# Attention's transposes taken two blocks of keys at a time: runs of eight, and one split of 1024 columns for two of 512

## The chip, the cores and the metric

The kernel runs on one core of one Trainium2 chip. The metric is the device time of one execution in microseconds (us), taken several times; the median counts.

## What is computed

A model of three stages: an attention block with its feed-forward network, a long-convolution block with its own, and a second block of a state-space branch and a pooling branch. Everything is float32. The change touches the attention alone, with 16 heads, 512 query rows and 768 keys (256 of a context, 512 of the sequence):

```python
def one_block(qblk):
    s = jnp.einsum('bqhd,bkhd->bhqk', qblk, k).astype(F32) * scale
    p = jax.nn.softmax(s, axis=-1).astype(v.dtype)
    return jnp.einsum('bhqk,bkhd->bqhd', p, v)
```

The queries and keys have 96 numbers per head, the values 64. The output of the heads is multiplied by `mla_w_o` and added to `x`; the kernel's later stages are the same before and after the change.

## The kernel before

Engines: PE is TensorE (matmuls and transposes), ACT is ScalarE, DVE is VectorE, and SP's queue issues the loads. A float32 operand of a matmul is split into a high part (ACT copies it to `fp32r`) and a low part (DVE subtracts the high part); the helper is `split`, and its two instructions carry the lines 262 (ACT) and 263 (DVE). A product takes three matmuls (lines 266 to 268) or, with packed values, two.

Per head `h` the attention does this:

- `proj_q`, `proj_k`, `proj_v` make the operands of later heads, in the PSUM tile `pj_pj` (one buffer, tag `pj`).
- `score(h, i)` makes the scores of 128 queries against 768 keys in `pss` (tag `sc`, two buffers of 1024 columns), takes the row maximum on DVE (line 890), the exponential on ACT (892), the reciprocal on DVE (893) and scales on ACT (897). The result is `p`, with queries on the partitions.
- `trans(h, j)` turns the block `j` of 128 keys, for the four blocks of queries: four PE transposes into the tile `pst` of 512 columns (tag `tr`, two buffers), and then `split` into `pth` and `ptl` (three buffers each). There are six blocks of keys per head.
- `pv_(h, j)` multiplies the packed values `v` with `pth` (line 914) and with `ptl` (915) into `pso` (tag `pso`), and after the last block adds the halves (919 on ACT, 920 on DVE).

The word list `STEPS` sets the order in which a head's calls are made: `s0` is `score(h+1, 0)`, `q0` the projection of a later head, `t2` is `trans(h, 2)`, `o3` is `pv_(h, 3)`, `M0` one call of `mod_row`. `mod_row` (line 385) belongs to another stage: it loads a row block `mr` of 512 KB, which SP issues, and reduces it on DVE (line 388); 24 such rows are put into the attention. `PPLAN` is the list for the first projections, with a letter for the PSUM tag each one uses.

The calls are traced in that order, and a scheduler then orders each engine's instructions by priority and by a model of when an operand is ready, so a later call's matmuls can stand between those of an earlier one. On the chip each engine works through its row in order and waits at semaphores.

From the last heads on, matmuls of the output projection (`ps_r`, with `h_wo`) stand among those of the attention.

Of the kernel before, what the change touches and what calls it, by code (L numbers as in the profile page):

```python
# [9 lines left out]
F32 = mybir.dt.float32  # L10
F32R = mybir.dt.float32r
# [7 lines left out]
L = 512  # L19
# [165 lines left out]
MR0 = [0] * 4  # L185
MR = [2] * 12 + [0]
XV, XK = 9, 9
PPLAN = "k1o k0t v0p S0 v2s v1s B0 E0 v5p q0s v3o q1t s0 v4p s1 s2 s3"
QPLAN = "a0 a1 k0 g0 r0 g1 y0 e1 e0 e2 l1 R0 g2 l0 Z0 z0 Y0 g3 l2"
STEPS = "s0 q0 t0 k0 t1 s1 o0 t2 o1 t3 o2 t4 M0 s2 o3 v0 t5 k1 v1 s3 M1 v2 x0 o4 o5"  # L190
PLAN = """F I9 F L0 L1 X0 X1 F m1 L2 L3 V F q0 q1 X2 X3 m3 F L4 L5 q2 q3 X4 X5 m5 F L6 L7 q4 q5 X6 X7 m7 F O0 q6 q7 S L8 L9 m9 R c0 F L10 L11 n0 n1 n2 n3
m11 L12 L13 n4 n5 n6 n7 m13 L14 L15 d0 F d1 W0 W1 W2 m15 O1 p0 d2 C0 C1 p1 F c1 C2 C3 d3 p2 K C4 C5 p3 d4 C6 C7 F p4 Q0 Q1 d5 Q2 Q3 p5 d6 Q4 Q5 Q6 Q7 p6 d7 T p7 U
N0 N1 N2 N3 D0 D1 N4 N5 D2 D3 N6 N7 D4 D5 D6 D7 F"""
# [2 lines left out]
def build(nc, tc, A, dbg=None):  # L196
    dbg = dbg or {}
    es = ExitStack()
    pe, act, dve = nc.tensor, nc.scalar, nc.vector
# [11 lines left out]
    ident = const.tile([128, 128], F32, name="ident")  # L211
# [17 lines left out]
    def opool(es_, name, bufs, **kw):  # L229
        kw["reuse_waits"] = "tile"  # L230
        return es_.enter_context(tc.tile_pool(name=name, bufs=bufs, **kw))
# [29 lines left out]
    def split(dsthi, dstlo, src):  # L261
        act.activation(dsthi, src, AF.Copy)  # L262
        dve.tensor_tensor(out=dstlo, in0=src, in1=dsthi.bitcast(F32), op=ALU.subtract)  # L263
# [118 lines left out]
    def gain(dst, sc, g):  # L382
        dve.scalar_tensor_tensor(out=dst, in0=sc, scalar=1.0, in1=g, op0=ALU.add, op1=ALU.mult)

    def mod_row(mpool, cb, n):
        raw = mpool.tile([128, 1024], F32, name="mr", tag="mr", bufs=2)
        nc.sync.dma_start(out=raw, in_=A["modT"][n - 16])
        dve.tensor_tensor_reduce(raw, raw, cb, 1.0, 0.0, ALU.mult, ALU.add, mods[:, n:n + 1])  # L388

# [3 lines left out]
    def load_cb(mpool):  # L393
        cb = mpool.tile([128, 1024], F32, name="cb")
        nc.sync.dma_start(out=cb, in_=A["crow"].broadcast_to([128, 1024]))
        act.activation(cb, cb, AF.Silu)
        return cb
# [11 lines left out]
    x0 = [rp.tile([128, L], F32, name=f"x0_{k}") for k in range(KT)]  # L409
# [8 lines left out]
    pp = opool(es_a, "pp0", 4, space=PSUM)  # L418
# [333 lines left out]
    rowp = opool(es_a, "row0", 1)  # L752
    cb = load_cb(rowp)
    rows = list(range(16, 40))
# [77 lines left out]
    pp = opool(es_ps, "ppa", 1, space=PSUM)  # L832
    ap_ = opool(ph, "ap", 2)
    rowp = opool(es_row, "rowp", 1, side="right")
    cb = load_cb(rowp)
    O = [op_.tile([128, L], F32, name=f"O{k}") for k in range(KT)]
    vt, Qt, Pt, Tt, Ot = {}, {}, {}, {}, {}

    def pjt(tag):
        return pp.tile([128, 1024 if tag == "sc" else L], F32, name="pj_" + tag, tag=tag, bufs=2 if tag in ("sc", "tr") else 1)[:, :L]  # L840

    def proj_v(qr, j, tag="pj"):
        uvh, uvl = wuv.block(qr)
        ps = pjt(tag)
        js = slice(j * 128, (j + 1) * 128)
        for k in range(2):
            w = slice(k * 256, (k + 1) * 256)
            pe.matmul(ps[:, :256], ckh[k][:, js], uvh[:, w], start=(k == 0), stop=False)
            pe.matmul(ps[:, :256], ckl[k][:, js], uvh[:, w], start=False, stop=False)
            pe.matmul(ps[:, :256], ckh[k][:, js], uvl[:, w], start=False, stop=(k == 1))  # L850
        v = ap_.tile([128, 4, 2, 64], F32R, name="v", bufs=12)
        p3 = ps[:, :256].rearrange("p (h d) -> p h d", h=4)
        act.activation(v[:, :, 0, :], p3, AF.Copy)
        dve.tensor_tensor(out=v[:, :, 1, :], in0=p3, in1=v[:, :, 0, :].bitcast(F32), op=ALU.subtract)
        vt[qr, j] = v

    def proj_k(h, part, tag="pj"):
        cs = (slice(0, L), KC)[part]
        w_ = cs.stop - cs.start
        psk = pjt(tag)  # L860
        for k in range(2):
            mm3(psk[:, :w_], wuk.unit(h + k), (ckh[k][:, cs], ckl[k][:, cs]), k == 0, k == 1)
        for e in range(2):
            b = (h + e) % 3
            act.activation(Kh[b][0:64, cs], psk[64 * e:64 * e + 64, :w_], AF.Copy)
            dve.tensor_tensor(out=Kl[b][0:64, cs], in0=psk[64 * e:64 * e + 64, :w_],
                              in1=Kh[b][0:64, cs].bitcast(F32), op=ALU.subtract)

    def proj_q(h, tag="pj"):
        psq = pjt(tag)  # L870
        chunk(psq, wuq, h * 4, cq, FULL)
        Qh = ap_.tile([128, L], F32R, name="Qh")
        Ql = ap_.tile([128, L], F32R, name="Ql")
        qf = ap_.tile([128, L], F32, name="qf", bufs=1)
        dve.tensor_tensor(out=qf, in0=psq, in1=qtab, op=ALU.mult)
        split(Qh, Ql, qf)
        Qt[h] = (Qh, Ql)

    def score(h, i):
        kb = h % 3  # L880
        Qh, Ql = Qt[h]
        qs = slice(i * 128, (i + 1) * 128)
        pss = pp.tile([128, 1024], F32, name="pss", tag="sc", bufs=2)
        for ks in (slice(0, L), KC):
            pe.matmul(pss[:, ks], Qh[:, qs], Kh[kb][:, ks], start=True, stop=False)
            pe.matmul(pss[:, ks], Qh[:, qs], Kl[kb][:, ks], start=False, stop=False)
            pe.matmul(pss[:, ks], Ql[:, qs], Kh[kb][:, ks], start=False, stop=True)
        st = const.tile([128, 4], F32, name="st", tag="st", bufs=6)
        nm, sm, rsm = st[:, 0:1], st[:, 1:2], st[:, 2:3]
        dve.tensor_reduce(out=nm, in_=pss[:, :NK], axis=AX.X, op=ALU.max, negate=True)  # L890
        p = ap_.tile([128, NK], F32, name="p", bufs=7)
        act.activation(p, pss[:, :NK], AF.Exp, bias=nm, accum_out=sm)
        dve.reciprocal(out=rsm, in_=sm)
        if (h % len(PS)) < len(PS) and i in PS[h % len(PS)]:
            dve.tensor_scalar(out=p, in0=p, scalar1=rsm, scalar2=None, op0=ALU.mult)
        else:
            act.activation(p, p, AF.Copy, scale=rsm)
        Pt[h, i] = p

    def trans(h, j):  # L900
        pst = pp.tile([128, L], F32, name="pst", tag="tr", bufs=2)
        for i in range(4):
            pe.transpose(pst[:, i * 128:(i + 1) * 128], Pt[h, i][:, j * 128:(j + 1) * 128], ident)  # L903
        pth = ap_.tile([128, L], F32R, name="pth", bufs=3)
        ptl = ap_.tile([128, L], F32R, name="ptl", bufs=3)
        split(pth, ptl, pst)
        Tt[h, j] = (pth, ptl)

    def pv_(h, j):
        if j == 0:  # L910
# [13 lines left out]
    tags = {"t": "tr", "o": "pso", "p": "pj", "s": "sc"}  # L924
    for t in PPLAN.split():
        i = int(t[1])
# [24 lines left out]
    def osplit(k):  # L951

        if k not in oh:
            oh[k] = ohp.tile([128, L], F32R, name=f"oh{k}")
            ol[k] = op_.tile([128, L], F32R, name=f"ol{k}", tag=f"O{k - 1}")
            split(oh[k], ol[k], O[k])
# [23 lines left out]
    for h in range(H):  # L980
        n1, n2 = h + 1 < H, h + 2 < H
        kk = n2 and h % 2 == 0
        vq = (h + 2) // 4 if (h % 4 >= 2 and h + 2 < H) else None
        for t in STEPS.split():
            j = int(t[1:])
            if t[0] == "s" and n1:
                score(h + 1, j)
            elif t[0] == "q" and n2:
                proj_q(h + 2)
            elif t[0] == "t":  # L990
                trans(h, j)
            elif t[0] == "k" and kk:
                proj_k(h + 2, j)
            elif t[0] == "o":
                pv_(h, j)
            elif t[0] == "v" and vq is not None:
                proj_v(vq, 3 * (h % 2) + j)
            elif t[0] == "x":
                if h % 4 == XV and h < 12:
                    wuv.load(h // 4 + 1)  # L1000
                if h == XK:
                    wuk.load(1)
            elif t[0] == "M" and j < MR[min(h, 12)]:
                mod_row(rowp, cb, rows.pop(0))
            if h > 13 and t[0] not in "Mx":
                next(fill, None)
        if h == 11:
            assert not rows
            es_row.close()
            ohp = opool(es_o, "ohp", 1, side="right")  # L1010
        if 10 < h < 15 and h % 2:
            for k in range(h // 2 + 1):
                osplit(k)
        if h == 13:
            wos = Stream(A["wo"], "wo")
            fill = wo_lead()
# [855 lines left out]
    class Final(Norm):  # L1872
# [33 lines left out]
        def turn(self, i, ks):  # L1906
            for b in self.blocks[i]:
                for k in ks:
                    if k % 4 == 0:
                        self.pt[b, k // 4] = pp.tile([128, 4, 128], F32, name="ps_r", tag="mm")  # L1910
                    pe.transpose(self.pt[b, k // 4][:, k % 4], xs[k][:, 128 * b:128 * b + 128], ident)
# [46 lines left out]
```

## Time and profile before

| | us |
|---|---|
| median of 3 runs (lowest, highest) | 1694.62 (1693.62, 1694.64) |
| the profiled execution, its own time | 1693.84 |
| its span in the profile | 1692.0 |
| PE busy | 1657.9 (98%) |
| DVE busy | 1210.3 (72%) |
| ACT busy | 832.9 (49%) |

Two matmuls overlap in the array, and the profile models their ends, so the busy time of PE hides short waits. The step from one start to the next tells more: a matmul of 512 columns has a duration of about 0.39 us, and the next one starts 0.23 us later. The attention lies between 130 us and 402 us of the span. Its first transpose starts at 154.12 us, its last run of transposes at 396.16 us.

### The profile page before, as it was taken

What the parts mean: (1) busy time and instruction counts of PE and PEld (TensorE: products, weight loads), DVE (VectorE), ACT (ScalarE), POOL (GpSimd) and SP (SyncE); (2) the same over time, 40 slices, a digit from 0 to 9 for tenths busy, and PEclk for the clock granted to TensorE, in tenths of its full rate; (3) what the DMA queues carried; (4) which work ended last, traced back from release to release, by engine and by line L of the source; (5) the groups of instructions that cost most, each with busy time, mean ns of one, the idle gap of its engine ahead of it and who ended that gap; (6) DMA issues with size and microseconds to landing.
All of it is one profiled execution on the core that took longest, in us unless ns stands there. A gap on an engine that the chain in (4) does not pass through costs nothing.

```text
span 1692.0 us, 22489 instructions
## 1 busy us (share of the span) xinstructions
PE 1657.9 (98%) x8637; PEld 1398.4 (83%) x8637; DVE 1210.3 (72%) x2042; ACT 832.9 (49%) x1286; POOL 0.9 (0%) x10
## 2 busy tenths in 40 slices
PE   6999999999999999999999999999999999999998
PEld 4687888878988888889888898888888898888887
DVE  6668999875899865645899879884585454937443
ACT  5577988884543324434533255442244345354233
POOL 0000000000000000000000000000000000000000
PEclk9999999999999999999999999999999999999999
DMA  7725231013487752232232332444442245533221
GB/s 264 263 95 168 94 106 63 26 56 107 160 277 273 268 203 100 95 102 103 100 100 92 115 112 88 147 133 153 146 150 100 98 152 168 190 98 112 100 87 51
DMA packets 91901, 224.88 MB, mean 133 GB/s; under 512 B 22764, under 2 KB 38384, under 8 KB 91665
## 3 DMA queue, kind: packets, MB, share of 16 engines
q1 hardware_dynamic: 91472, 223.41, 39.1%
q8 instruction: 68, 1.11, 0.3%
q14 instruction: 41, 0.33, 0.1%
q10 hardware_dynamic: 320, 0.04, 0.0%
HBM read 206.66 MB, written 16.74 MB: 132 GB/s over the span
## 4 chain that ended last, share of the span: by engine, by line
PE 90%; DVE 4%; ACT 4%; issue 1%; DMA 1%; ACTq 0%; DVEq 0%; SPq 0%
PE ps_r L266 7%; PE ps_r L267 7%; PE ps_r L268 7%; PE psg L268 5%; PE psg L266 5%; PE psg L267 5%; PE psa L268 4%; PE psa L266 4%; PE psa L267 4%; PE psp L266 4%; PE psp L267 4%; PE psp L268 4%; PE pst L903 2%; PE pac L524 1%; PE pso L914 1%; PE pso L915 1%
## 5 line engine op out<-in xcount | busy, mean ns | idle before, releaser
L247 ACT ACTIVATE h_up<-r_up 128x1024 fp32r<-128x1024 f32 x88 | 92.9, 1057 | 145.8 <-PE psg L267 82.3
L266 PE MATMUL ps_r<-mh,h_dn 128*128 128x512 f32 (+1 forms) x407 | 146.9, 361 | 0.0
L267 PE MATMUL ps_r<-ml,h_dn 128*128 128x512 f32 (+1 forms) x407 | 146.7, 361 | 0.0
L268 PE MATMUL ps_r<-mh,l_dn 128*128 128x512 f32 (+1 forms) x407 | 146.6, 360 | 0.0
L248 DVE TENSOR_TENSOR l_up<-r_up,h_up 128x1024 fp32r<-128x1024 f32 x88 | 107.3, 1219 | 52.4 <-ACT h_up L247 51.1
L268 PE MATMUL psg<-hh,l_up 128*128 128x512 f32 x336 | 133.0, 396 | 0.0
L266 PE MATMUL psg<-hh,h_up 128*128 128x512 f32 x336 | 131.7, 392 | 0.0
L267 PE MATMUL psg<-hl,h_up 128*128 128x512 f32 x336 | 131.5, 391 | 0.0
L268 PE MATMUL psa<-hh,l_up 128*128 128x512 f32 x320 | 126.0, 394 | 0.0
L266 PE MATMUL psa<-hh,h_up 128*128 128x512 f32 x320 | 124.7, 390 | 0.0
L267 PE MATMUL psa<-hl,h_up 128*128 128x512 f32 x320 | 124.5, 389 | 0.0
L388 DVE CUSTOM_DVE_ANT_0 mr<-mr,cb 128x1024 f32<-128x1024 f32 x80 | 96.9, 1217 | 22.4 <-DMA mr<-modT 20.4
L247 ACT ACTIVATE h_dn<-r_dn 128x1024 fp32r<-128x1024 f32 x44 | 46.5, 1058 | 102.9 <-PE ps_r L267 66.2
L266 PE MATMUL psp<-hh,h_win 128*128 128x512 f32 x232 | 92.4, 398 | 0.0
L268 PE MATMUL psp<-hh,l_win 128*128 128x512 f32 x232 | 90.4, 390 | 0.0
L267 PE MATMUL psp<-hl,h_win 128*128 128x512 f32 x232 | 90.3, 389 | 0.0
L248 DVE TENSOR_TENSOR l_dn<-r_dn,h_dn 128x1024 fp32r<-128x1024 f32 x44 | 53.6, 1220 | 48.2 <-ACT h_dn L247 48.2
L267 PEld LDWEIGHTS ps_r<-ml,h_dn 128*128 128x128 f32 x407 | 76.8, 189 | 11.7
L268 PEld LDWEIGHTS ps_r<-mh,l_dn 128*128 128x128 f32 x407 | 76.8, 189 | 11.6
L266 PEld LDWEIGHTS ps_r<-mh,h_dn 128*128 128x128 f32 x407 | 76.8, 189 | 11.6
L1179 ACT ACTIVATE og<-og 128x512 f32<-128x512 f32 x44 | 27.8, 632 | 111.5 <-DVE og L1136 109.9
L263 DVE TENSOR_TENSOR ptl<-pst,pth 128x512 fp32r<-128x512 f32 x96 | 63.6, 682 | 16.0 <-ACT pth L262 15.6
(656 smaller groups left out, 4472.8 us busy)
## 6 DMA issues: line engine op xcount, KB each, us to landing
r_up<-wup SPq DMA_DIRECT2D x88, 512.0 KB, 3.3
mr<-modT SPq DMA_DIRECT2D x80, 512.0 KB, 4.0
r_dn<-wdn SPq DMA_DIRECT2D x44, 512.0 KB, 3.2
r_win<-win SPq DMA_DIRECT2D x32, 512.0 KB, 3.2
r_hyin<-hyin SPq DMA_DIRECT2D x24, 512.0 KB, 3.2
rmod<-mod SPq DMA_DIRECT2D x16, 512.0 KB, 6.2
x<-xT SPq DMA_DIRECT2D x16, 256.0 KB, 4.6
Hd<-hq SPq DMA_DIRECT2D x8, 512.0 KB, 3.5
```

Source lines behind the costliest of these rows:

```text
L247: act.activation(hi, raw, AF.Copy)
L248: dve.tensor_tensor(out=lo, in0=raw, in1=hi.bitcast(F32), op=ALU.subtract)
L263: dve.tensor_tensor(out=dstlo, in0=src, in1=dsthi.bitcast(F32), op=ALU.subtract)
L266: pe.matmul(ps, w[0], a[0], start=start, stop=False)
L267: pe.matmul(ps, w[0], a[1], start=False, stop=False)
L268: pe.matmul(ps, w[1], a[0], start=False, stop=stop)
L388: dve.tensor_tensor_reduce(raw, raw, cb, 1.0, 0.0, ALU.mult, ALU.add, mods[:, n:n + 1])
L524: pe.matmul(ps, tabs[:, o * 128:(o + 1) * 128], ta[r], start=(i == 0), stop=(i == len(terms) - 1))
L903: pe.transpose(pst[:, i * 128:(i + 1) * 128], Pt[h, i][:, j * 128:(j + 1) * 128], ident)
L914: pe.matmul(Ot[h], vw, pth, start=(j == 0), stop=False)
L915: pe.matmul(Ot[h], vw, ptl, start=False, stop=(j == 5))
L1179: act.activation(og, og, AF.Silu)
```

## The change

`trans` now serves two blocks of keys. Its PSUM tile `pst` has 1024 columns (two banks) and one buffer, where there were two of 512. Eight transposes fill it; the first is placed by the scheduler, and the other seven are tied behind it with a high priority, so that they follow as soon as their operands allow. One `split` of 1024 columns follows on ACT and one on DVE. `pth` and `ptl` have two buffers of 1024 columns, where there were three of 512.

The lists follow: `STEPS` has `t0`, `t2` and `t4`, each ahead of its two `o`. In `PPLAN` the projection `k0` uses a buffer of tag `sc`, as `tr` has only one. To make room in SBUF, the values `v` have 10 buffers for 12, and the row block `mr` of `mod_row` has one for two within the attention.

```diff
-PPLAN = "k1o k0t v0p S0 v2s v1s B0 E0 v5p q0s v3o q1t s0 v4p s1 s2 s3"
+PPLAN = "k1o k0s v0p S0 v2s v1s B0 E0 v5p q0s v3o q1t s0 v4p s1 s2 s3"
-STEPS = "s0 q0 t0 k0 t1 s1 o0 t2 o1 t3 o2 t4 M0 s2 o3 v0 t5 k1 v1 s3 M1 v2 x0 o4 o5"
+STEPS = "s0 q0 t0 k0 s1 o0 o1 M0 t2 v0 s2 o2 o3 k1 v1 t4 s3 M1 v2 x0 o4 o5"
...
-    def mod_row(mpool, cb, n):
-        raw = mpool.tile([128, 1024], F32, name="mr", tag="mr", bufs=2)
+    def mod_row(mpool, cb, n, bufs=2):
+        raw = mpool.tile([128, 1024], F32, name="mr", tag="mr", bufs=bufs)
...
-        v = ap_.tile([128, 4, 2, 64], F32R, name="v", bufs=12)
+        v = ap_.tile([128, 4, 2, 64], F32R, name="v", bufs=10)
...
     def trans(h, j):
-        pst = pp.tile([128, L], F32, name="pst", tag="tr", bufs=2)
-        for i in range(4):
-            pe.transpose(pst[:, i * 128:(i + 1) * 128], Pt[h, i][:, j * 128:(j + 1) * 128], ident)
-        pth = ap_.tile([128, L], F32R, name="pth", bufs=3)
-        ptl = ap_.tile([128, L], F32R, name="ptl", bufs=3)
+        pst = pp.tile([128, 2, L], F32, name="pst", tag="tr")
+        def turn(n):
+            e, i = n // 4, n % 4
+            return pe.transpose(pst[:, e, i * 128:(i + 1) * 128], Pt[h, i][:, (j + e) * 128:(j + e + 1) * 128], ident)
+        first = turn(0)
+        with tc.issue_after(first.ins), tc.high_priority(offset=2000):
+            for n in range(1, 8):
+                turn(n)
+        pth = ap_.tile([128, 2, L], F32R, name="pth")
+        ptl = ap_.tile([128, 2, L], F32R, name="ptl")
         split(pth, ptl, pst)
-        Tt[h, j] = (pth, ptl)
+        for e in range(2):
+            Tt[h, j + e] = (pth[:, e], ptl[:, e])
...
-                mod_row(rowp, cb, rows.pop(0))
+                mod_row(rowp, cb, rows.pop(0), 1)
```

The rows that differ lie in the attention alone; behind it each engine has the same rows in both kernels. In PE's row the 384 transposes stood in 115 runs, of which 72 had four; now they stand in 52, of which 45 have eight.

PE, third head, its first pair of blocks of keys (`Kh`, `Qh` are the next head's operands). Before, a run of four and what follows it up to the next run:

```order
L903 MATMUL pst<-ident,p 128x128 x4
L885 MATMUL pss<-Kh_873,Qh 128x512
L886 MATMUL pss<-Kl_876,Qh 128x512
L887 MATMUL pss<-Kh_873,Ql 128x512
L885 MATMUL pss<-Kh_873,Qh 128x256
L886 MATMUL pss<-Kl_876,Qh 128x256
L887 MATMUL pss<-Kh_873,Ql 128x256
L914 MATMUL pso<-pth,v 128x512
L885 MATMUL pss<-Kh_873,Qh 128x512
L886 MATMUL pss<-Kl_876,Qh 128x512
L887 MATMUL pss<-Kh_873,Ql 128x512
L915 MATMUL pso<-ptl,v 128x512
```

The same place now:

```order
L906 MATMUL pst<-ident,p 128x128 x8
L885 MATMUL pss<-Kh_873,Qh 128x512
L886 MATMUL pss<-Kl_876,Qh 128x512
L887 MATMUL pss<-Kh_873,Ql 128x512
L885 MATMUL pss<-Kh_873,Qh 128x256
L886 MATMUL pss<-Kl_876,Qh 128x256
L887 MATMUL pss<-Kh_873,Ql 128x256
L924 MATMUL pso<-pth,v 128x512
L885 MATMUL pss<-Kh_873,Qh 128x512
L925 MATMUL pso<-ptl,v 128x512
L924 MATMUL pso<-pth,v 128x512
L925 MATMUL pso<-ptl,v 128x512
```

The run is twice as long, one matmul of scores stands between the first products with `pth` and `ptl` where three stood, and the next row is the next run of eight.

DVE, in the first two heads, two reductions of `mod_row` (`ISA mr`) that follow each other closely (`st` belongs to the softmax, `qf` and `Kl` to projections), before:

```order
L388 ISA mr,mods<-mr,cb 128x1024
L388 ISA mods 128x1
L893 RECIPROCAL st<-st 128x1
L875 TENSOR_TENSOR qf<-pj_pj,qtab 128x512
L890 TENSOR_REDUCE st<-pss 128x1
L388 ISA mr,mods<-mr,cb 128x1024
```

Two that follow each other closely there now:

```order
L388 ISA mr,mods<-mr,cb 128x1024
L388 ISA mods 128x1
L893 RECIPROCAL st<-st 128x1
L890 TENSOR_REDUCE st<-pss 128x1
L263 TENSOR_TENSOR ptl<-pst,pth 128x1024
L866 TENSOR_TENSOR Kl_878<-pj_pj,Kh_875 64x256
L388 ISA mr,mods<-mr,cb 128x1024
```

More work stands between them than before, and a split of 1024 columns is part of it.

## Rows read from the trace of the kernel before

**Rows 1.** The page, part 4: the chain's shares of the span.

```profile
PE 90%; DVE 4%; ACT 4%; issue 1%; DMA 1%; ACTq 0%; DVEq 0%; SPq 0%
```

**Rows 2.** Timeline of PE, attention's first and last transposes: start, us, instruction, count.

```profile
154.12 0.60 PE L903 MATMUL pst<-ident,p 128*128 128x128 f32 x4
...
396.16 0.60 PE L903 MATMUL pst<-ident,p 128*128 128x128 f32 x4
```

**Rows 3.** Chain in order of time, middle of attention: start, us, piece.

```profile
244.90 0.22 PE pst L903 x2
...
249.27 0.44 PE pst L903 x4
...
252.31 0.12 PE pj_pj L850
252.43 0.24 PE pso L915
```

**Rows 4.** Windows, attention's halves: busy us (count) of PE, PEld, DVE, ACT, POOL.

```profile
153.00:290.00 137.00, 134.85 (x782) 112.89 (x782) 131.68 (x237) 124.09 (x226) 0.00 (x0) 1.00 0.30 102
290.00:398.00 108.00, 106.70 (x593) 87.49 (x592) 77.95 (x136) 84.54 (x152) 0.00 (x0) 1.00 0.13 45
```

**Rows 5.** Waits of PEld, 153 to 398 us: total us, times, longest.

```profile
PEld pso L915 <- DVE ptl L263: 2.7, 9, 0.6
PEld pso L914 <- ACT pth L262: 2.0, 8, 0.4
```

**Rows 6.** Timelines around one run late in attention: PE, ACT, DVE.

```profile
392.48 0.60 PE L903 MATMUL pst<-ident,p 128*128 128x128 f32 x4
...
393.12 0.60 ACT L262 ACTIVATE pth<-pst 128x512 fp32r<-128x512 f32 x1 [1.70 <-PE pst L903]
...
393.75 0.69 DVE L263 TENSOR_TENSOR ptl<-pst,pth 128x512 fp32r<-128x512 f32 x1 [1.61 <-ACT pth L262]
```

**Rows 7.** Groups by shape (page, and 153 to 320 us): busy us, mean ns, idle before.

```profile
L262 ACT ACTIVATE Qh<-qf 128x512 fp32r<-128x512 f32 x11 | 6.9, 630 | 0.0
L262 ACT ACTIVATE pth<-pst 128x512 fp32r<-128x512 f32 x66 | 38.0, 594 | 5.1 <-PE pst L903 4.7
L247 ACT ACTIVATE h_up<-r_up 128x1024 fp32r<-128x1024 f32 x88 | 92.9, 1057 | 145.8 <-PE psg L267 82.3
L263 DVE TENSOR_TENSOR ptl<-pst,pth 128x512 fp32r<-128x512 f32 x66 | 43.7, 681 | 2.4 <-ACT pth L262 2.0
L248 DVE TENSOR_TENSOR l_up<-r_up,h_up 128x1024 fp32r<-128x1024 f32 x88 | 107.3, 1219 | 52.4 <-ACT h_up L247 51.1
L890 DVE TENSOR_REDUCE st<-pss 128x1 f32<-128x768 f32 x46 | 43.4, 943 | 1.9 <-PE pss L887 1.5
L892 ACT ACTIVATE p<-pss,st 128x768 f32<-128x768 f32 x46 | 41.4, 902 | 1.8 <-DVE st L890 1.4
```

**Rows 8.** Timelines of DVE and ACT: two splits of 512 in a row.

```profile
217.96 1.27 DVE L263 TENSOR_TENSOR ptl<-pst,pth 128x512 fp32r<-128x512 f32 x2
...
217.09 1.08 ACT L262 ACTIVATE pth<-pst 128x512 fp32r<-128x512 f32 x2
```

**Rows 9.** Timelines of PEld and PE: a product that waited for its split.

```profile
250.89 0.19 PEld L914 LDWEIGHTS pso<-pth,v 128*128 128x128 f32 x1 [0.16 <-ACT pth L262]
...
250.89 0.50 PE L914 MATMUL pso<-pth,v 128*128 128x512 f32 x1
251.23 0.28 PE L886 MATMUL pss<-Kl,Qh 128*128 128x256 f32 x1
```

**Rows 10.** Rows `mr`: timelines of DVE and SP, and the tile's landing times.

```profile
204.41 1.20 DVE L388 CUSTOM_DVE_ANT_0 mr<-mr,cb 128x1024 f32<-128x1024 f32 x1
206.21 1.20 DVE L388 CUSTOM_DVE_ANT_0 mr<-mr,cb 128x1024 f32<-128x1024 f32 x1
...
215.88 1.21 DVE L388 CUSTOM_DVE_ANT_0 mr<-mr,cb 128x1024 f32<-128x1024 f32 x1
...
217.13 0.33 SPq L387 DMA_DIRECT2D mr<-modT  x1
...
DMA to landing us min/median/max: 3.1/4.0/5.2
```

More of the change, by code (lines that the diff above doesn't have):

```diff
@@ L839, in pjt @@
     def pjt(tag):
-        return pp.tile([128, 1024 if tag == "sc" else L], F32, name="pj_" + tag, tag=tag, bufs=2 if tag in ("sc", "tr") else 1)[:, :L]
+        return pp.tile([128, 1024 if tag in ("sc", "tr") else L], F32, name="pj_" + tag, tag=tag, bufs=2 if tag == "sc" else 1)[:, :L]
     def proj_v(qr, j, tag="pj"):
```

## The prediction

> **What bounds the kernel now.** I read the chain of the page first: 90% of the end's path is PE [rows 1]. So the change is worth what it does to PE's row in the attention. The timeline then gives that stretch: from the first transpose (154.12 us) to the last run's start (396.16) are 242.0 us [rows 2]. The chain in order of time gives the steps of a full PE row: 0.23 us for 512 columns, 0.12 for 256, and 0.44 for a run of four transposes, 0.22 for a run of two [rows 3]. So a transpose costs 0.109 us in either, and a run has no start-up price to save. PE's row holds, from the first run to the last one's start, 644 matmuls of 512 columns, 330 of 256 and 380 transposes. At 0.231, 0.118 and 0.109 us that is 148.8 + 38.9 + 41.4 = 229.1 us. **The other 12.9 us are waits**, and they are all that this change can win or enlarge.
>
> The windows split the waits over two regimes: DVE is busy 131.7 of 137 us in the first half (96%), but 78.0 of 108 (72%) in the second [rows 4]. By the same steps PE's work is 129.5 us in the first half and 102.7 in the second (each matmul counted in the half in which it starts), so the waits are 7.5 of 137 and 5.3 of 108: 5.5% and 4.9%. They are hardly rarer where DVE has time to spare. So most of them come from the length of chains and the order in which ACT and DVE take them; the waits of the weight loads for `pth` and `ptl`, 2.0 and 2.7 us [rows 5], are a part.
>
> **What is removed.** PE's matmuls stay the same. 63 fewer starts of a run save nothing on PE, by the two prices above. ACT and DVE lose 48 instructions each. Two splits of 512 queued back to back take 1.27 us on DVE and 1.08 on ACT [rows 8]; one of 1024 takes 1.219 on DVE, and on ACT 1.057 from SBUF. ACT reads PSUM a little faster (594 against 630 ns for 512 columns), which makes 594 + (1057 - 630) = 1.02 us [rows 7]. So DVE gets back 0.05 to 2 x 0.681 - 1.219 = 0.14 us per pair, 2.4 to 6.9 us over 48 pairs, and ACT 0.06 to 0.17. None of it is on the path by itself; it shortens the queue on DVE, at most 27 x 0.14 = 3.8 us in the half where that queue is full.
>
> **What is added: a longer chain from a run to its products.** Late in attention, where ACT and DVE are free, the rows show it bare. The run starts at 392.48 and is through at 392.92; ACT starts at 393.12, 0.20 later, and takes 0.60; DVE starts 0.03 after ACT and takes 0.69 [rows 6]. `pth` is there 0.80 us behind the run, `ptl` 1.52. With 1024 columns it is 0.20 + 1.02 = 1.22 us for `pth` and 1.22 + 0.03 + 1.22 = 2.47 for `ptl`. The next run needs the same 2.47 us, because `pst` has one buffer now and DVE reads it last. A run and its chain then take 0.87 + 2.47 = 3.34 us, three times a head, of about 15 us.
>
> I laid these needs against PE's row. Before, PE has enough work behind each of the 96 blocks: the least is 0.90 us ahead of `pth` and 1.59 ahead of `ptl`. Now 21 of the 48 pairs lack something. The place in the order that was shown is typical: six matmuls of scores, 3 x 0.231 + 3 x 0.118 = 1.05 us, stand ahead of `pth`, and two more 512s, 1.51 us, ahead of `ptl`, which needs 2.47. **It lacks 0.96 us.** Five pairs lack 0.84 to 1.19 (the 7th, 12th, 19th, 31st and 42nd), together 5.0; sixteen lack up to 0.5, together 2.3. That is 7.3 us if ACT and DVE take each split at once, so it is a floor for these waits. A wait also costs the step behind it: a product that waited for `pth` was followed by the next matmul after 0.34 us, not 0.23 [rows 9]. 21 x 0.11 = 2.3, **in sum 9.6 us**.
>
> The scores' buffers lose distance too: twice a score follows only 1.28 us behind the second last one, whose maximum and exponential take 0.20 + 0.94 + 0.90 = 2.04 [rows 7], and once 1.99: 1.6 us. The tile `pj` lacks about 1.2 in four places. Some of this falls into the waits above; of 2.8 I take 1.5, with 0 and 2.8 as ends.
>
> **`mr` with one buffer.** A row's load is issued as its buffer's last reduction ends (215.88 + 1.21, issue at 217.13) and lands 3.1 us later at the least; with two buffers reductions can still follow each other after 1.8 us [rows 10]. With one they need 1.21 + 0.04 + 3.1 = 4.35 us from start to start. In DVE's row now most gaps hold 4.4 us of work or more, but seven hold 3.3 to 4.2 (the shown one 3.6: 1.21 + 0.94 + 1.22 and two short ones), and lack 4.9 us together. DVE waits there with splits and maxima queued behind it, and PE behind those; SP's later loads wait behind the issue, with room, since the weights come a head ahead. DVE's own idle moments stretch the gaps, so I take 1, with 0 and 4.9 as ends.
>
> `v` with 10 buffers: head by head the old blocks are free before the new ones are written, no cost. `PPLAN`: the same matmuls and the same tail of that row, 0, give or take 0.5.
>
> **What stays of the old waits** is the open term, between nothing and all 12.9 us. For nothing speaks that PE's new stops give ACT and DVE time to catch up, and the shorter queue. For all speaks that the waits are as common where DVE is 72% busy. I take half, 6.5.
>
> The sum of waits: 9.6 + 1.5 + 1 + 6.5 = 18.6 us for 12.9, **+5.7 us**; behind the last run all stays as it was. The span of 1692.0 stands in an execution of 1693.84, and the median is 1694.62; the 1.84 us around the span don't change. I predict 1694.6 + 5.7 = 1700.3 us.
>
> A rule bears on this. In the Trainium skill, "Perfetto Trace Analysis", section Optimizing Scalar/DVE Operations, grouping into larger operations pays where the engine is saturated, and where ACT and DVE are not saturated but make bubbles on others, breaking operations up lets work end sooner. By its first half 27 merges gain in the first regime; by its second half the other 21 lose. The rows show both regimes, and the floor of 9.6 us falls into both (4.6 us of the bare lacks up to the 27th pair, 2.8 behind it), so I side with the second.
>
> **The rivals.**
> *Faster:* the first half is DVE's, and PE's lacks there only replace waits that it has anyhow; the merges are then a gain of up to 3.8 us, and the second half keeps its time. 1694.6 - 3.8 = 1691 us, or 1688 if ACT's relief counts as well. For it speaks the 96%, against it that the second half loses its bare 2.8 + 9 x 0.11 = 3.8 us. It decides from where less than 3 us of the old waits remain. 17%.
> *No change:* the old waits vanish almost wholly into the new ones, 9.6 + 1.5 + 2 = 13 for 12.9: 1694.6, give or take 3. 22%.
> *Slower still:* `mr` holds DVE by its whole 4.9 us, and all the old waits remain: 9.6 + 2.8 + 4.9 + 12.9 = 30.2, +17.3, 1711.9 at the very end; half of this excess gives 1706. 11%.
> The forecast itself, 1698 to 1705, has 50%.
>
> **How the numbers follow.** About 0.2%, 3.4 us, is what a measurement of this kernel can tell from no change. Slower by more: 50 + 11 = 61%; same 22%; faster 17%. The range goes from 1691.5, where the gainful rival begins, to 1708.5; it leaves out most of the 17% and a little of the 11%.
>
> **What would show it.** In the changed profile: runs of eight at 0.87 us; a split of 1.02 us on ACT and 1.22 on DVE; the weight loads' waits for `ptl` and `pth` grown from 4.7 us to 9 or more; a repeated gap of about a us behind the 7th, 19th and 31st run; DVE waiting for `mr`'s load in the first half, where it hardly did. The forecast is wrong if the stretch from the first transpose to the last run takes less than 242 us, and its term for the old waits is wrong if the waits for `pj` and the scores go to zero or stay whole.

## The result, and the profile after

| | before | after |
|---|---|---|
| median of 4 runs | 1694.26 us (1693.62 to 1694.64) | 1719.52 us (1717.65 to 1721.59) |
| ratio | | 1.015 (95% interval 1.0138 to 1.0162) |
| span of the profiled execution | 1692.0 us | 1715.9 us |
| first transpose of attention | 154.12 | 154.01 |
| start of the last run of transposes | 396.16 | 417.11 |
| PE takes up `Wo` again behind attention | 401.14 | 423.55 |

The change makes the kernel slower by 25.3 us. I had forecast 5.7 us, with 1708.5 as the end of the range. Even the rival "slower still" ended at 1711.9. The direction was right, the size far off.

The page's part 4 of the changed kernel, the chain's shares of the span (before: [rows 1]):

```profile
PE 86%; ACT 7%; DVE 5%; issue 1%; DMA 0%; ACTq 0%; DVEq 0%
```

PE gave up four points of the chain to ACT and DVE. The timeline of PE, the first and the last transposes of attention (columns as in [rows 2]):

```profile
154.01 0.38 PE L906 MATMUL pst<-ident,p 128*128 128x128 f32 x2
...
417.11 1.04 PE L906 MATMUL pst<-ident,p 128*128 128x128 f32 x8
```

The stretch from the first transpose to the last run's start took 242.0 us and takes 263.1 now: **21.1 of the 23.9 us by which the span grew lie there**. The waits, for 153 to 420 us of the changed kernel (who waited for whom, total us, times, longest; before, for two of them: [rows 5]):

```profile
ACT p L892 <- PE pst L906: 15.6, 12, 3.2
...
PEld pso L925 <- DVE ptl L263: 11.6, 18, 1.1
PEld pss L885 <- ACT p L892: 11.1, 17, 1.2
...
PEld pso L924 <- ACT pth L262: 9.2, 21, 0.8
...
DVE mr L388 <- DMA mr<-modT: 0.9, 3, 0.5
```

The scores' row in the kernel before, 153 to 398 us:

```profile
PEld pss L885 <- ACT p L892: 1.1, 4, 0.4
```

The weight loads of the products wait 20.8 us where they waited 4.7, and those of the scores 11.1 where they waited 1.1. A score waits there because both of its PSUM buffers are still held by exponentials that ACT hasn't done. And the exponentials have a wait that the kernel before didn't have: 15.6 us for a run of transposes, which must be through before one of the seven `p` buffers is free. In all twelve places it is the third run of a head, the last that reads its four `p`. Reckoned in PE's row, as what is above the steps of [rows 3], the waits ahead of products went from 5.0 to 18.0 us and those ahead of scores from 5.5 to 15.5. The rises, 13 and 10 us, are the 21 us and a little more; waits ahead of `pj_pj` fell by about 4. How a step next to a run of transposes is counted shifts the figures for the scores by up to 2 us, not the rises. All waits of the stretch, by the count of the prediction, are 35.1 us now (263.1 less 641 x 0.231, 330 x 0.118 and 376 x 0.109) for the old 12.9; 1.1 us of work now stands behind the last run's start.

The groups by shape show the new splits as costed, 1.02 and 1.22 us (153 to 420 us; busy us, mean ns, idle before; before: [rows 7]):

```profile
L263 DVE TENSOR_TENSOR ptl<-pst,pth 128x1024 fp32r<-128x1024 f32 x48 | 58.6, 1220 | 19.3 <-ACT pth L262 19.0
...
L262 ACT ACTIVATE pth<-pst 128x1024 fp32r<-128x1024 f32 x48 | 49.0, 1021 | 15.0 <-PE pst L906 14.6
```

The rest of the loss lies at attention's end. The chain in order of time (start, us, piece; short pieces left out):

```profile
417.27 0.89 PE pst L906 x8
418.18 1.04 ACT pth L262
419.24 1.24 DVE ptl L263
420.52 0.50 PE pso L925
421.25 0.25 PE pso L925
421.52 0.60 ACT ot L929
422.15 0.70 DVE O L930
422.87 0.64 ACT oh L262
423.55 0.96 PE ps_r L266 x3
424.51 0.43 PE ps_r L267
```

A run of eight takes 0.87 to 0.89 us. Its `pth` and `ptl` are there 1.22 and 2.47 us behind it: the bare chain is the one that was forecast. Here all of it lies on the path, so from the last run's start to `Wo` it is 6.44 us for 4.98. Then the matmuls take 0.43 us each and not 0.23. The windows show the granted clock there (busy us and count of PE, PEld, DVE, ACT, POOL; PEclk; DMA share; GB/s), of the changed kernel:

```profile
424.00:428.00 4.00, 4.00 (x12) 3.02 (x11) 2.57 (x4) 3.03 (x4) 0.00 (x0) 0.57 0.00 0
```

and of the kernel before at the same work:

```profile
402.00:406.00 4.00, 4.00 (x19) 3.25 (x19) 3.25 (x5) 3.59 (x5) 0.00 (x0) 1.00 0.10 15
```

The clock stood at its lower level, 1.2 GHz, for most of that window, 8 matmuls by 0.20 us = 1.6 us. In sum 21.1 + 1.5 + 1.6 - 0.1 (the first transpose) = 24.1, about the 23.9 of the span. The medians are 25.3 us apart; the other 1.4 us stand in no trace.

### The profile page after: what moved, and what is told of

The parts are those of the page before. It is cut to its first block, busy times and chain, and to the rows that moved or that the text cites. A ratio compares the mean times of both kernels' runs of the same rounds, so it can differ in the third digit from the quotient of the medians.

```text
span 1715.9 us, 22387 instructions
## 1 busy us (share of the span) xinstructions
PE 1667.3 (97%) x8637; PEld 1402.3 (82%) x8637; DVE 1209.4 (70%) x1994; ACT 831.3 (48%) x1238; POOL 0.9 (0%) x10
## 4 chain that ended last, share of the span: by engine, by line
PE 86%; ACT 7%; DVE 5%; issue 1%; DMA 0%; ACTq 0%; DVEq 0%
PE ps_r L267 7%; PE ps_r L266 7%; PE ps_r L268 7%; PE psg L268 5%; PE psg L266 4%; PE psg L267 4%; PE psa L268 4%; PE psa L266 4%; PE psa L267 4%; PE psp L266 4%; PE psp L268 4%; PE psp L267 4%; PE pac L524 2%; PE pst L906 1%; ACT p L892 1%
## 5 line engine op out<-in xcount | busy, mean ns | idle before, releaser
L267 PEld LDWEIGHTS psg<-hl,h_up 128*128 128x128 f32 x336 | 63.1, 188 | 13.2
```

Source lines behind the costliest of these rows:

```text
L267: pe.matmul(ps, w[0], a[1], start=False, stop=False)
```

## The experiments

### Which part of the change is it?

The kernel before was timed beside each (1693.6 to 1694.4 us); differences are to that. Two theories stood at first. **W**: the split of 1024 columns from one `pst` makes the chain long, and all else follows. **P**: the runs of eight hold the `p` buffers, and ACT's exponentials wait for them. Four kernels take a part each.

*Splits of 512 in the changed kernel:*

```diff
-        split(pth, ptl, pst)
         for e in range(2):
+            split(pth[:, e], ptl[:, e], pst[:, e])
             Tt[h, j + e] = (pth[:, e], ptl[:, e])
```

> The changed kernel, but each pair's split is cut at the bank: ACT and DVE each take two operations of 512 columns, as before the change; runs of eight, one pst of two banks and the order list stay. Theory W (the split of 1024 makes the chain from a run to its products long, 1.22 and 2.47 us behind the run): the first products have their operands after 0.80 and 1.5 us again, the products' waits of 18 us on PE go back to some 5 to 8, and the time falls by 9 to 14 us to 1706-1711. Theory P (the p tiles are held too long by the runs of eight, so that ACT's exponentials wait for them, 15.6 us, and the scores behind): the scores' waits of 15.5 us stay, and the time falls by 3 at most, to 1716-1720.

Measured: 1721.28 us, no gain. That is no answer on W, for the waits (150 to 430 us) have a new one:

```profile
ACT pth L262 <- DVE ptl L263: 10.2, 12, 2.0
```

ACT's split of the second bank starts behind the end of DVE's split of the first in all 48 pairs. The two share the tile `pst`, though not the bank, and the tile `pth`; which of the two makes ACT wait the run doesn't tell. The chain got longer and not shorter: the products' weight loads wait 29.1 us there and 21.3 in the changed kernel, in the same window.

*Eight `p` buffers in the changed kernel* (`v` nine for ten, `ot` in `qf`'s buffer):

```diff
-        p = ap_.tile([128, NK], F32, name="p", bufs=7)
+        p = ap_.tile([128, NK], F32, name="p", bufs=8)
```

> The changed kernel with eight p buffers for seven; for the room, v has nine buffers for ten and ot shares qf's buffer. Theory P: no exponential waits for a transpose any more (15.6 us in 12 places before), PE's waits at the scores go from 15.5 us back to about 5.5, and some of the waits for pth that queue behind the exponentials go too: 1703-1710. Theory W: the exponentials waited beside work that was late anyhow, and the time stays within 3 us, 1717-1722.

Measured: 1719.63 us. The exponentials' wait for transposes fell to 1.9 us, yet the time stayed: P falls as the main cause. Here too the scheduler made a new order, so a kernel with the order held follows below.

*The order list alone, in the kernel before:*

```diff
-STEPS = "s0 q0 t0 k0 t1 s1 o0 t2 o1 t3 o2 t4 M0 s2 o3 v0 t5 k1 v1 s3 M1 v2 x0 o4 o5"
+STEPS = "s0 q0 t0 t1 k0 s1 o0 o1 M0 t2 t3 v0 s2 o2 o3 k1 v1 t4 t5 s3 M1 v2 x0 o4 o5"
```

> The kernel before with the new order list alone: t0 t1, t2 t3 and t4 t5 stand next to each other where t0, t2 and t4 stand in the new list; runs of four, two pst of 512 columns, splits of 512, all buffers as before. If the list is the cause (scores and projections at other places), it loses 10 us or more: above 1704. If the pairing in one tile is the cause (by W or P), it stays near the time before: 1692-1698.

Measured: 1701.09 us, +6.7. Between the two; neither theory had it.

*The small parts alone, in the kernel before* (`mr` one buffer in attention, `v` ten, `k0` in a buffer of tag `sc`):

> The kernel before with the small parts of the change alone: one mr buffer for two in the attention, v with ten buffers for twelve, k0 in a buffer of the scores. Both theories: within 0.2%, 1692-1697. The rival by which mr's single buffer holds DVE: up to 4.9 us more, 1697-1700.

Measured: 1700.88 us, +6.5, while DVE waited only 1.5 us for `mr`. The scheduler had put all of attention into a new order.

### The order held fast

So a change of buffers also changes the order, and the two have to be taken apart. The following kernels carry a table with the place of every instruction of PE, ACT and DVE in attention, and edges of order (no waits) from each to the next:

```diff
+        row = [mine[int(r)] for r in ranks.split()]
+        for a, b in zip(row, row[1:]):
+            tc.add_manual_dep(b, a.name, mybir.DependencyInfo(mybir.DependencyClass.NoSync, mybir.DependencyReason.DATA), reason="order")
```

*One `mr` buffer and ten `v`, in the old order:*

> One mr buffer in the attention and ten v buffers, as in the run of the small parts, but PE, ACT and DVE keep, instruction by instruction, the order of the kernel before (edges of order from a table; k0 stays in its old buffer). In the run of the small parts the scheduler had made a new order, and it lost 6.5 us. Theory O (the new order costs, not the buffers): the loss goes, 1693.5-1697, and what stays is DVE's wait for mr's load, 1.5 us in that run. Theory R (a single mr buffer stops DVE): the 6.5 us stay, 1699-1702.

Measured: 1719.0 us, **+24.8**. Theory O falls for this part, and R was far too mild. The waits, 150 to 430 us:

```profile
DVE mr L388 <- DMA mr<-modT: 14.5, 7, 3.5
```

In the old order the single buffer stops DVE seven times, and PE pays more than DVE waited. Part of that is PE's clock. In the profiled execution it fell to its lower level, 1.2 GHz, near 152, 221, 255 and 292 us, each time behind a stop of PE of 2.5 to 3.2 us. The first of these places (columns as in [rows 4]):

```profile
149.00:152.40 3.40, 1.02 (x7) 0.72 (x6) 3.40 (x7) 2.47 (x4) 0.00 (x0) 0.99 0.42 154
152.40:155.80 3.40, 3.40 (x10) 2.63 (x9) 2.63 (x6) 3.39 (x7) 0.00 (x0) 0.50 0.30 107
```

There a matmul of 512 columns follows after 0.43 us and not 0.23. By the steps of PE's row that is 1.3 to 1.5 us at each place and 5.6 us in all. In the kernel before the clock stayed at 1.00 through all of attention.

In the changed kernel DVE's row for `mr` says 0.9 us: there the scheduler had spread the reductions. So here the new order is the scheduler's answer to a new need, not an accident beside it.

*Splits of 512 and two `pst` of one bank, in the changed kernel's order:*

```diff
-        pst = pp.tile([128, 2, L], F32, name="pst", tag="tr")
+        pst = [pp.tile([128, L], F32, name="pst", tag="tr", bufs=2) for _ in range(2)]
...
+            split(pth, ptl, pst[e])
```

> The changed kernel with PE's, ACT's and DVE's order kept as it is there, but with two pst of one bank each and splits of 512 columns, two per engine where one of 1024 stood. In the run of the halves each second half on ACT waited for DVE's first, since both read one PSUM tile, and the order was a new one; this run has neither. Theory C (the long chain of the wide split costs): the first products have their operands 0.4 and 1.0 us sooner; of the products' 18 us of waits at least half go: 1704-1711. Theory O (the order costs): the waits only move on, 1715-1720.

Measured: 1711.51 us, 8.0 less than the changed kernel. Its waits, 150 to 430 us:

```profile
PEld pss L885 <- ACT p L892: 15.0, 20, 1.6
...
PEld pso L925 <- DVE ptl L263: 5.7, 16, 0.7
...
PEld pso L924 <- ACT pth L262: 2.6, 4, 0.7
```

The products' waits fall from 21.3 us (the changed kernel in this window) to 8.3, as C said. The scores' waits don't fall; they grow from 11.1 to 15.0.

*The pairs in the old order*, each run of eight and each wide split where the first of its two stood, with one `mr` buffer:

> The changed kernel (runs of eight in one pst, splits of 1024, its buffers), but PE, ACT and DVE keep the order of the kernel before: each run of eight stands where the first run of four of its pair stood, each wide split where the first of its two splits stood. By the bare chain (1.22 and 2.47 us behind a run) PE's row lacks 7.7 us ahead of the products with pth and 7.8 ahead of those with ptl in this order, 15.5 together, where it lacks 7.3 in the changed kernel's own order. Theory C: the loss is that of the chain, 15.5 and some of the old 12.9 us of waits, so 1707-1716, and this order is worse for pairs than their own by the bare sum. Theory O: the old order is better by itself in what ACT and DVE do, and this run stands nearer to the kernel before, 1700-1707.

Measured: 1739.17 us, outside of both, since it holds the single `mr` buffer's price in that order as well (DVE waits 14.3 us for it). With two `mr` buffers, and the stage ahead in the new order:

> The pairs in the old order again (1739.2 with a single mr buffer), now with two mr buffers, and the stage ahead of the first transposes in the order of the changed kernel. That takes the waits for mr's load away (14.3 us of DVE there; the single buffer cost the kernel before 24.8 us in its own order) and leaves the pairs alone. Theory C: the bare lack of 15.5 us on PE, and part of the old waits: 1707-1716. If the pairs cost more than their bare chain: 1717 or more.

Measured: 1719.83 us, +25.7: more than the bare chain. The waits, 150 to 430 us:

```profile
PEld pso L925 <- DVE ptl L263: 15.3, 22, 2.2
PEld pso L924 <- ACT pth L262: 15.1, 24, 1.1
...
PEld pss L885 <- ACT p L892: 4.5, 6, 1.2
```

**In the old order the pairs cost the same 25 us as in their own, but at the products**: 30.4 us there, 4.5 at the scores.

*Two `mr` buffers and `k0` in its old buffer, in the changed kernel, order free:*

> The changed kernel without two of its small parts: mr has two buffers in the attention again, and k0 uses the buffer of the transposes; the order is made anew by the scheduler. Theory R (the single mr buffer costs): 5 us or more come back, below 1714.5. Theory C and O: DVE waited only 0.9 us for mr's loads, so no more than 1 us comes back by the buffer, and the new order moves the time by a few us either way, 1714-1723.

Measured: 1725.68 us, slower by 6 than with the single `mr` buffer. R falls for the changed kernel.

*Eight `p` buffers, order of the changed kernel:*

> The changed kernel with eight p buffers for seven, and PE's, ACT's and DVE's order kept as it is there, row for row (for the room v has nine buffers and ot uses a tile of an earlier stage; in the first run with eight p buffers the order was a new one, and ot shared a buffer with qf). Theory P: the exponentials' 15.6 us of waits for a run of transposes go, the scores' 15.5 us on PE fall to 8 or less, and the time falls by 5 to 9 us, to 1710-1714. Theory A (ACT and DVE are late anyhow at these places): the exponentials wait for their maxima or their turn instead, and the time stays at 1717-1721.

Measured: 1716.36 us, 3.2 less. No exponential waits for transposes any more, and the scores' loads wait 7.9 us for 11.1; `pth` and `ptl` wait as before. P has a share of 3 us.

*Both together, and a second `mr` buffer besides:*

> The splits of 512 with two pst, as in the run of halves in the changed kernel's order (1711.5), and eight p buffers as well; order kept. Theory P: the scores' waits, 19.4 us in that run, fall by half or more: 1698-1704. Theory A: no more than 2 us go, 1709-1712.

> As the run with splits of 512, two pst and eight p buffers, with two mr buffers besides; order kept. Now every buffer and every operation is as in the kernel before or better, and only the order and the runs of eight are those of the change. The time of this run less that of the kernel before is what the new order costs by itself. Theory O puts 5 us or more on it (1699 or above); by theories C and P it is within 3 us of the kernel before (1691-1697). The second mr buffer by itself: no more than 1 us against the run without it.

Measured: 1710.11 and 1711.2 us. So in this order 17 us stay although no split is wider than before and no buffer of the disputed ones is fewer. (`v` has nine; the run of the same program in the old order, below, bounds what that can cost.)

### What in that order?

My next theory, **N**: in the new order normalizations (`p<-p`, 0.93 us) stand ahead of exponentials that are ready. An edit of ACT's row puts the exponentials first.

> As the run with all buffers (1711.2: splits of 512, two pst, eight p, two mr, the changed kernel's order), with one edit in ACT's row: at the 17 places where an exponential was ready and a normalization of an earlier score (0.93 us) that had not begun stood ahead of it, the exponential goes ahead. DVE's and PE's rows stay. Theory N (the new order lets scores follow each other so that exponentials queue behind normalizations on ACT, and the two score buffers stay taken): up to 17 x 0.93 = 15.8 us of lateness go, PE's waits at the scores, 16 us, fall by a third or more, and the time falls by 4 to 9 us, to 1702-1707. Theory S (the scores are late by the whole of ACT's row, or the normalizations that now come later hold the transposes instead): within 2 us, 1709-1713.

Measured: 1717.72 us, 6.5 slower. The waits of this kernel, 150 to 430 us:

```profile
PEld pso L925 <- DVE ptl L263: 7.2, 20, 0.7
PEld pss L885 <- ACT p L892: 7.2, 10, 1.1
...
PEld pso L924 <- ACT pth L262: 4.6, 4, 1.3
```

and of the one without the edit:

```profile
PEld pss L885 <- ACT p L892: 11.1, 13, 1.6
...
PEld pso L925 <- DVE ptl L263: 5.7, 16, 0.7
...
PEld pso L924 <- ACT pth L262: 2.2, 4, 0.7
```

The scores' waits fell by 3.9 us, the products' rose by 3.9, and transposes and projections waited besides. N falls: in this row of PE the edit of ACT's row gained nothing.

> The same edit in ACT's row on the changed kernel with eight p buffers (1716.4: splits of 1024, one pst, one mr). Theory N: 4 to 9 us faster, 1707-1712. Theory S: 1714-1718.

> The kernel before, its order kept but for the 5 places where an exponential was ready and a normalization that had not begun stood ahead of it: there it goes ahead. Theory N: the kernel before has few such places, and gains at most 5 x 0.93 us, 1690-1694. Theory S: no difference, 1693-1697.

Measured: 1725.65 us (9 slower), and 1694.45 us beside 1693.62 for the kernel before (ratio 1.0006, 0.9997 to 1.0016): no difference. Some 6 of the 9 us are clock, an estimate from the steps of PE's row: in the profiled execution with the edit the granted clock fell five times from 150 us on, behind stops of PE of 1.7 to 2.2 us, without it once, and each time cost about 1.4 us. The edit still gains nothing.

### The order free, the operations as before

*All buffers and operations as in that last program, but the rows of the kernel before:*

> The same program as the run with all buffers in the changed kernel's order (1711.2), instruction for instruction, with one difference: from the first transposes on, PE, ACT and DVE have the order of the kernel before (runs of four again). If the order of the rows is what the 17 us are, this run is back at the kernel before: 1692-1697. If something in the buffers or in the table of order edges costs, it is 1699 or more.

Measured: 1697.99 us (ratio 1.0023, 1.0013 to 1.0033), between the two ranges. So nine `v` and all else in this program cost 3.8 us in the old order. The same instructions take 13 us less in the old order than in the changed kernel's.

*Runs of eight, tied, with the new list, two `pst`, splits of 512 and two `mr`; order free:*

> The new order list and the runs of eight tied behind their first transpose, but with all buffers and operations of the kernel before (two pst of one bank, splits of 512, two mr, k0 in its old buffer; v has ten buffers, pth and ptl four of 512): the run of the list alone (1701.1) with the tie added, the scheduler free. If runs of eight cost by themselves (all four p of a head and both pst at once, ACT and DVE get their splits in bunches): 1706-1712. If only the wide splits with one pst cost: 1699-1703.

Measured: **1696.96 us** (ratio 1.0015, 1.0006 to 1.0024). Runs of eight, their tie and the new list cost nearly nothing. This kernel and the one with two `mr` buffers and `k0` in its old buffer (1725.68) differ in how a pair is held and split (two `pst` of one bank and splits of 512 into tiles of their own, against one `pst` of two banks and splits of 1024) and in the order that the scheduler then makes, and in nothing else. **That is 28.7 us**, with the scheduler free in both. About 2 us of it are clock: from 130 us on the lower level stands for 13.7 us in the profiled execution of the wide one, and for 6.8 in that of the narrow one. The waits, 150 to 430 us, of the wide one:

```profile
ACT p L892 <- PE pst L906: 15.2, 14, 3.2
...
PEld pso L925 <- DVE ptl L263: 11.6, 20, 1.0
...
PEld pso L924 <- ACT pth L262: 10.2, 28, 1.1
...
PEld pss L885 <- ACT p L892: 9.1, 12, 1.5
```

and of the narrow one, which has no line of the first kind:

```profile
PEld pso L925 <- DVE ptl L263: 3.1, 8, 0.6
PEld pso L924 <- ACT pth L262: 3.0, 10, 0.3
...
PEld pss L885 <- ACT p L892: 2.2, 5, 0.8
```

All three kinds of wait go together, those of the scores too.

*The changed kernel without the tie:*

> The changed kernel without the tie: each of the eight transposes is placed by the scheduler by itself; with one pst most still stand in runs of eight (45 of 49). The order is made anew. If the tie holds scores or projections off PE at bad moments, 4 us or more come back: below 1715.5. If the wide split and its one pst set the time whatever the order: 1717-1726.

Measured: 1717.55 us. The tie is not it.

So the kernels fall into two groups. With one two-bank `pst` and wide splits, seven kernels give 1716.4 to 1725.7 us (the changed kernel; two `mr`; untied; the old order with two `mr`; eight `p`, with a new order, with the changed kernel's, and with exponentials first). The halves from one `pst` (1721.28) stand with them, though their splits are narrow. With two `pst` and splits of 512, an order made for them or the old one gives 1694 to 1701 (a single `mr` in the old order apart, here as in the first group); only the order that was made for the wide splits, put on narrow ones, gives 1710 to 1712, or 1717.7 once edited. With the scheduler free the groups are 16 us apart at the nearest (1717.55 and 1701.09), more than orders differ within either. None beats the kernel before.

What isn't separated: the width of the split from the single `pst` (the halves have narrow splits and one `pst`, but a wait of their own). Scores, transposes, `pj` and `pso` take all eight banks, so a second `pst` of two banks couldn't be tried. Nor do the runs tell why the scheduler's order for the wide splits moves the waits to the scores.

## Why the prediction failed, step by step

**Right:** no start-up price of a run (eight take 0.87); the splits' 1.02 and 1.22 us; the bare chain of 1.22 and 2.47; no gain to be seen from DVE's merges; waits of `ptl` and `pth` "from 4.7 to 9 or more" (20.8); side with the rule that breaks operations up. The gaps behind the 7th, 19th and 31st run are there: the product with `pth` follows the matmul ahead of it after 0.91 us behind the 7th and 19th, where the step behind 256 columns is 0.12, and the one with `ptl` after 1.26 behind the 31st. But behind the 7th and 19th the next stop, 1.35 us for a step of 0.23, is a score's, where the prediction had the product with `ptl` wait.

**The products' waits, 9.6 plus half of the old 5.0, made 12.1; they are 18.0.** The lacks were laid out with the bare chain, "a floor"; I then used the floor as the value. The row of ACT shows what a floor leaves out. Behind the 21st run, which is through at 267.82 (start, us, instruction, what it waited for), ACT:

```profile
267.70 0.90 ACT L892 ACTIVATE p<-pss,st 128x768 f32<-128x768 f32 x1 [0.17 <-PE pst L906]
...
268.71 0.38 ACT L865 ACTIVATE Kh<-pj_pj 64x256 fp32r<-64x256 f32 x1
269.12 1.03 ACT L262 ACTIVATE pth<-pst 128x1024 fp32r<-128x1024 f32 x1
```

DVE and PE:

```profile
269.68 0.96 DVE L890 TENSOR_REDUCE st<-pss 128x1 f32<-128x768 f32 x1
270.55 1.21 DVE L263 TENSOR_TENSOR ptl<-pst,pth 128x1024 fp32r<-128x1024 f32 x1
```

```profile
271.82 0.50 PE L925 MATMUL pso<-ptl,v 128*128 128x512 f32 x1 [0.80 <-DVE ptl L263]
```

ACT takes the split 1.3 us behind the run and not 0.2, since an exponential that had itself waited for this run's transposes, and a projection's piece, stand ahead; DVE takes its half behind a maximum. `ptl` is there 3.9 us behind the run, not 2.47. ACT and DVE are not free at such places, and a longer operation also delays whatever is queued behind it.

**The scores' waits, 1.5 (0 to 2.8) plus half of the old 5.5, made 4.2; they are 15.5.** This is the largest error, 11 us. I looked at the distance of scores in PE's row and took their exponentials as prompt (2.04 us). I didn't ask what the last run of a head sets free: its four `p`, of which the next exponentials need one. That wait, 15.6 us on ACT, is on no line of the prediction. Yet by itself it was worth only 3.2 us. Between the two free orders, 28.7 us apart, the scores' waits went with the wide split and its single `pst`; in the changed kernel's order narrow splits left them at 15.0 us. By what way the wide pair reaches the scores stays open.

**`mr`, 1 (0 to 4.9):** 0.9 us of waits in the changed kernel, right there. The bound of 4.9 holds for the changed kernel's row, on which it was reckoned, and for no other: in the old order nine gaps between reductions hold 1.8 to 3.7 us of DVE's work for the 4.35 needed, and a single buffer made DVE wait 14.5 us there and the kernel take 24.8 us more, 5.6 of them by the clock.

**"Behind the last run all stays":** wrong by 1.5 us, the longer chain laid bare, and by 1.6 of clock in the profiled execution, behind a stop of PE that the kernel before has too.

**Half of the old waits, 6.5:** how much of them stayed the trace can't tell, since old and new waits stand in the same rows.

**The sum:** 6 at the products, 11 at the scores, 3 behind the last run, less 1 for `mr`: about 19 us, for the 18.2 between the forecast rise of 5.7 us and the 23.9 of the span. So what failed are the sizes of two terms, the waits at the products and, above all, at the scores, where the exponentials' wait for a head's last run was put at nothing. The rival "faster" is refuted: whatever a DVE that was 96% busy gained from shorter work, the time doesn't show it. The windows of the changed kernel (columns as in [rows 4]) have it idler, not PE fuller:

```profile
153.00:300.00 147.00, 135.80 (x755) 110.39 (x754) 131.25 (x211) 121.05 (x196) 0.00 (x0) 1.00 0.30 102
300.00:420.00 120.00, 113.06 (x617) 92.26 (x616) 77.85 (x115) 86.77 (x134) 0.00 (x0) 1.00 0.12 40
```

DVE is busy 89% of the first stretch where it had 96%, and PE 92% where it had 98%.

Two rules of the Trainium skill stand beside this. "Perfetto Trace Analysis", section Optimizing Scalar/DVE Operations, says that grouping can help on a saturated engine, and breaking up where ACT and DVE aren't saturated but make bubbles on others. Here DVE was nearly saturated in the first half and the bubbles still decided, 25 us against at most 6.9 of saved work. The Trainium skill, "Perfetto Trace Analysis", section Optimizing Tensor Performance, says that independent matmul groups should rotate through different PSUM banks, so that evacuation overlaps the next group; the two kernels that are 28.7 us apart differ in that and in the width of the split, and agree with it as far as the two can't be told apart.

## What to carry to other kernels

Before merging two evacuations into one, write down how long the last of them holds its PSUM buffer and every operand of what fills it (here the `p` tiles), and what is queued behind it on each engine; here 48 merges saved 0.1 us of engine time each and cost 0.5 us each (25.3 / 48). A floor from bare latencies is not a forecast: where engines work in order and are as busy as here (DVE 72 to 96%), take the queue ahead of each link from the trace. And where a scheduler sets the order, try a change of buffers both with the order free and with it held, since it turns a wait at one place into a wait at another.

## What the runs showed of the hardware that I had not expected

- An engine's stop spreads: 14.5 us of DVE's waiting for loads in attention made the kernel 24.8 us longer, and 5.6 of these were four stretches at the lower clock behind stops of PE.
- PE stood 2.06 us ahead of `Wo`'s restart in both kernels. In the profiled execution of the changed kernel the granted clock then showed 0.57 for 4 us, in that of the kernel before 1.00; what sets the two apart the runs don't show. In all twenty profiled executions the last product and the restart start 2.45 to 2.56 us apart; in eleven the granted clock fell about there, in nine it didn't. Through the runs of eight of the changed kernel it stayed at 1.00 in both windows of attention; in eight of the other kernels, six of them with runs of eight, it fell within attention, behind stops of PE of 1.1 to 3.2 us.
- The same instructions in another order took 1698.0 or 1711.2 us, and orders that the scheduler made anew for much the same work lay 3 to 7 us above the kernel before.
